# A hybrid decoder step on one core: the order of a tile's scores and transposes, of a few splits and of several loads is changed

## The chip, the core and the metric

The kernel runs on one core of a Trainium2 chip. The core has a matrix engine (TensorE, PE in the profile; its weight loads are PEld), three engines for element-wise work (VectorE, DVE; ScalarE, ACT; GpSimd, POOL), and SyncE (SP), which here only issues DMA transfers. Each engine works through its own queue in order, and semaphores hold an instruction until what it needs is there. The metric is the time of one execution on the device in microseconds; the lower, the better.

## The reference

One layer of a decoder, for a prompt of 2048 tokens and a sample batch of 8 x 8 tokens, d_model 1024, all in float32:

```python
h = rms_norm(x, g_mix_pre)
proj = einsum('btd,de->bte', h, w_in)            # q, k, v | gq, gk, gv, gr, low-rank gate
attn = swa_banded(rope(q), rope(k), v, sinks)    # window 128, 8 q heads, 2 kv heads, hd 64
log_a = log_sigmoid(glr @ w_gk2 + b_gk) / 16
o, s_new = gla_chunked(gq, gk, gv, log_a, s0)    # 4 heads, dk 64, dv 128
gla_out = rms_norm(o, g_gla) * silu(gr)
x = x + rms_norm(concat(attn, gla_out) @ w_out, g_mix_post)
h = rms_norm(x, g_ffn_pre)
f = relu(h @ w_up) ** 2 @ w_down                 # d_ff 4096
x = x + rms_norm(f, g_ffn_post)
```

The key and value windows and the recurrent states are returned too.

## The kernel before

**Precision.** TensorE multiplies in a rounded float32 format (float32r). So every operand is split in two: a high part (ScalarE copies with rounding) and a low part (VectorE subtracts the high part from the source). A product is three matmuls: high x high, high x low, low x high. Most lines of the profile that read `hi` and `lo`, `o0` and `o1`, `wh` and `wl`, `kh` and `kl`, `ph` and `pl` are such pairs.

**Order.** The program is fully unrolled. A scheduler places each engine's instructions, and takes from those that are ready the one that stands first in the text. Two things bind it. The wrappers `te`, `ac` and `dv` (class InOrder) keep every TensorE, ScalarE and VectorE instruction issued through them in the order of the text; plain `nc.scalar`, `nc.vector`, `nc.gpsimd` and `nc.sync` (DMA) calls may be placed earlier. And `tc.issue_after(ins)` puts what a block issues on the engine of `ins` behind `ins` in that engine's queue; it doesn't touch instructions of other engines. So a block of DMAs (SP) after a matmul (PE) is not bound by it, and one after a DMA is.

**Stages.** In order of time: sliding-window attention with its part of the input projection (to about 325 us of the span); gated linear attention with the rest of the projection; output projection, norms and residual; the up projection of the first half of the tokens (rows 0 to 1023 and the sample, `sb` = 0), the down projection of that half, and both again for the second half. Up and down are products of 2 x 2 blocks with seven instead of eight multiplications, so sums and differences of blocks are made on VectorE beside them.

**Attention.** The main loop runs over 16 tiles of 128 tokens (i), and in each over four units (u): a unit is two query heads of one key head. `unit` is a generator; each `next` issues one step:

1. the sink column (GpSimd); 2. scores `sc`, four matmuls; 3. mask and minimum (VectorE, `s<-sc,amask,sink`); 4. exponentials (ScalarE); 5. reciprocal (VectorE) and normalization, on VectorE, but in unit 3 on ScalarE (`s<-s,den`); 6. transposes `pT`; 7. `ph` (ScalarE); 8. `pl` (VectorE); 9. product with the values, `av`; 10. `rest` (ScalarE); 11. the addition `mo` (VectorE).

Tile 0 has one key block instead of two: step 10 then writes mo directly and there is no step 11. Three units are under way at a time: `behind` (steps 8 to 11), `now` (3 to 7), `ahead` (1 and 2). `fill` is the stream of projection matmuls that are put between them; A_FILL says how many where. The PSUM banks that matter: tag d (one buffer) holds the transposed queries pq of the next tile, and then the transposed inputs xT, which therefore wait for the last reader of pq, the `ql<-pq,ql` subtraction.

`heads_T` (L406) transposes the next tile's heads and returns pieces that A_PLAN places: `lo0` and `lo1` subtract the low parts of keys (`kl`, then GpSimd copies them to the other half) and queries (`qh`/`ql`) for each key head, `hi1` makes a high part. `rest` and `vl` in the plan are take_rest (L345) and its subtractions: `qk`, `glr`, `vv` on ScalarE, then `vv`, `glr` on VectorE. `split_some` splits weights of the next stage, of which a GpSimd product, a ScalarE copy and a GpSimd subtraction are made for each; A_SPLIT says how many in which unit. After tile 15 come four sample units (L531).

**Gated attention.** `decays` (L945) makes the log decays (Abs, Exp, Ln on ScalarE), `level_sums` sums them in seven levels, `gate` (L961) makes the output gate with four ScalarE activations. `gla` yields numbers: so many matmuls of `fill` (the remaining projection) are issued there.

**Output projection.** L1527 goes through the tiles in B_ORDER. `load_mix` loads a tile's mixed inputs `mt` into one of two buffers and splits them.

**Up projection.** `up` (L1612) takes 16 chunks of w_up. For the first one `opening` (L1731) lays the splits and sums by hand between the products; `last_rows` is the residual of the last tile. `sum_down` (L1600) makes differences of w_down blocks in two halves a chunk, placed by DOWN_SUMS and `downs`. `sample_features` at the end of a chunk reads the bank `sam` into `samq`.

**Down projection.** `down` (L1945) goes through 7 x 16 units: each loads two raw operands (`down_raw`: `rs` from s_d, `rt` from t_d or w_down, three buffers each), splits them (`o0`, `o1`) and does 12 matmuls `dn`. `fetch_h` and `load_h` bring the joint inputs H of the second half in meanwhile, `finish` and `prepare_last` end the rows.

Of the kernel before, what the change touches and what calls it, by code (L numbers as in the profile page):

```python
# [21 lines left out]
P = 128  # L22
# [29 lines left out]
DOWN_SUMS = (4, 6, 8, 10)  # L52
# [5 lines left out]
A_LEAD, A_SPLIT, A_PL_FIRST = 14, (2, 1, 0, 0), ()  # L58
A_PLAN = [(name, (int(at[0]), at[1])) for name, at in dict(
    first="1B", hi1="3B", x1="1B", lo1="0A", x0="0C", rest="3A", lo0="3A", junk="2A", turn="1A", rstd="1A", vl="3B"  # L60
# [80 lines left out]
def hybrid_step_kernel(ctx: ExitStack, tc: tile.TileContext, I, O):  # L141
# [264 lines left out]
    def heads_T(i):  # L406
# [36 lines left out]
        def lo(r):  # L443
            dv.tensor_tensor(kl[half_of[r], r, 1, :], pk[half_of[r]], f32(ks[half_of[r], r, 1, :]), op=ALU.subtract)
            nc.gpsimd.tensor_copy(kl[half_of[1 - r], r, 1, :], f32(kl[half_of[r], r, 1, :]))
            dv.scalar_tensor_tensor(
# [4 lines left out]
            "lo0": lambda: lo(0),  # L451
            "hi1": lambda: ac.activation(qs[1][half_of[1]], pq[half_of[1]], AF.Copy, scale=-0.125),
            "lo1": lambda: lo(1),
# [170 lines left out]
    def load_consts():  # L624
# [19 lines left out]
        def part(n, shape, dtype):  # L644
# [3 lines left out]
            nc.vector.tensor_copy(t.rearrange("p a b -> p (a b)") if len(shape) > 1 else t, src)  # L648
# [136 lines left out]
    for i in range(NB):  # L785
# [34 lines left out]
        for u in range(4):  # L820
            for unit_ in (behind, now) if u in A_PL_FIRST else (now, behind):
                next(unit_, None)
            next(now)
            do(u, "A")
            later = next(queue)
# [3 lines left out]
            next(behind, None)  # L829
# [9 lines left out]
            if u == 3:  # L839
                next(now)  # L840
                next(behind, None)
                next(ahead)
            else:
                next(behind, None)
                next(ahead)
                next(now)
            do(u, "B")
            split_some(A_SPLIT[u] if i < NB - 1 else 1)
# [96 lines left out]
    def decays(i, n, before, kind="d"):  # L945
# [12 lines left out]
        nc.scalar.activation(t, t, AF.Ln, bias=1.0)  # L958
# [122 lines left out]
    def gla(i, gp, og=iter(())):  # L1081
# [9 lines left out]
        yield G_FILL[0] if i else 24, True  # L1091
# [18 lines left out]
        sg = gate(i, gp, P)  # L1110
# [248 lines left out]
    wo, pre, ogs_of, mixes, late_mix, put = {}, {}, {}, {}, [], []  # L1359
# [5 lines left out]
    for i in range(NB):  # L1365
        parts = [gla(i, gps[i], ogs_of.pop(i - 1, iter(())))]
        if i == 0:
            parts = [(n or (12, True) for n in decayed(i)), *parts]
# [158 lines left out]
    for n, i in enumerate(B_ORDER[2:]):  # L1527
        early.append((i, []))
        mixing = out_projecting(nc.tensor, i, early[-1][1])
        run(mixing, 24 if i == B_ORDER[-1] else 48)  # L1530
        if n == 0:
# [80 lines left out]
    def up(sb, fc, before, steps=iter(())):  # L1612
# [62 lines left out]
        def downs(p):  # L1675

            if sb == 0 and fc > 1 and p in ((1, 2, 4) if fc in DOWN_SUMS else (1, 2)):
                sum_down(*next(down_halves))
# [52 lines left out]
    def opening(p, taken, ahead):  # L1731
# [5 lines left out]
        elif p == 2:  # L1737
            taken(p)
            next(last_rows)
            run(load_h(0, 6, ac, dv))  # L1740
            U.pop("tmp").release()
        elif p == 8:
            taken(p)
            sums_24(0, 0, dv)
            split_sums(0, 0, 24, ac, dv)
# [49 lines left out]
    def down_raw(sb, p, fc, which):  # L1795
# [10 lines left out]
        nc.sync.dma_start(raw, src)  # L1806
# [138 lines left out]
    def down(sb):  # L1945
# [28 lines left out]
        for n, (p, fc) in enumerate(units):  # L1974
# [3 lines left out]
            if sb == 0 and (p, fc) in fetched:  # L1978
                fetch_h(1, fetched[p, fc])
# [141 lines left out]
```

## Time and profile before

| | us |
|---|---|
| median of 3 runs | 2227.38 (2225.35 to 2230.99) |
| profiled execution | 2234.79 |
| its span, first to last instruction | 2233.0 |
| mean granted TensorE clock | 0.993 |
| ScalarE, VectorE and GpSimd busy | 1219.5, 1521.8, 261.0 |
| DMA | 419.92 MB, 188 GB/s over the span |

A row of the timeline reads: start, duration, engine, line, operation, out<-in by the program's names, shapes, count, and in brackets the idle time of the engine just before and what ended it. Most operations run through a helper, and so carry line L130; they are told apart by their tiles. A row of the list of waits reads: who waited for whom, the sum in us, how often, the longest. Matmuls are pipelined: successive starts tell how long one occupies the array, durations overlap.

### The profile page before, as it was taken

The page shows a single profiled execution, that of the slowest core. Times are in us where ns is not written, and L with a number is a line of the kernel's source. Part 1 is how long each engine was busy: PE and PEld are TensorE (multiplying, and loading weights), DVE is VectorE, ACT ScalarE, POOL GpSimd, SP SyncE. Part 2 cuts the span into 40 slices and gives each one's busy share as a digit, 9 for nine tenths or more (in the row PEclk, how much of TensorE's full clock was granted, in tenths as well). Part 3 has the DMA queues.
Part 4 walks back from the last instruction along what each step waited for, and adds up shares of the span by engine and source line. Part 5 has one row for each costly group of instructions (what it writes and reads, how often), then busy time and mean ns, then how long its engine had stood idle before and what let it go on. Part 6 is the DMA issues. An engine that isn't in the chain of part 4 may idle for free.

```text
span 2233.0 us, 34187 instructions
## 1 busy us (share of the span) xinstructions
PE 2174.4 (97%) x11784; PEld 1868.1 (84%) x11784; DVE 1521.8 (68%) x3101; ACT 1219.5 (55%) x2626; POOL 261.0 (12%) x417
## 2 busy tenths in 40 slices
PE   8999999999999999999999999999999999999998
PEld 7888888999998887788888778888888888888886
DVE  5778866777876565788888755447776666555566
ACT  5788866556665444455555554335454444454444
POOL 3566422111121110000000000000000000000000
PEclk9999999999999999999999999999999999999999
DMA  7334332124346559967786887557644444766674
GB/s 234 120 125 138 103 103 69 50 85 140 112 149 211 192 177 314 311 225 253 263 271 235 279 272 233 184 182 240 206 168 155 156 156 146 266 200 194 197 255 151
DMA packets 242313, 419.92 MB, mean 188 GB/s; under 512 B 26132, under 2 KB 142332, under 8 KB 238028
## 3 DMA queue, kind: packets, MB, share of 16 engines
q1 hardware_dynamic: 242140, 417.74, 56.0%
q8 instruction: 93, 1.52, 0.3%
q14 instruction: 80, 0.66, 0.1%
HBM read 270.53 MB, written 148.18 MB: 188 GB/s over the span
## 4 chain that ended last, share of the span: by engine, by line
PE 77%; ACT 7%; DVE 7%; DMA 5%; issue 2%; POOL 0%; SPq 0%; DVEq 0%; ACTq 0%; POOLq 0%
PE dn L130 24%; PE gproj L130 9%; PE uc L130 7%; PE ua L130 7%; PE out L1269 6%; PE ub L130 4%; PE ud L130 4%; PE ue L130 4%; PE proj L130 2%; ACT s L130 2%; PE sam L130 1%; PE dsam L130 1%; PE o L130 1%; DMA rt<-t_d 1%; DVE s L130 1%
## 5 line engine op out<-in xcount | busy, mean ns | idle before, releaser
L130 PE MATMUL dn<-o0t,o0s 128*128 128x512 f32 x896 | 350.1, 391 | 2.5 <-DVE samq L130 1.9
L130 PE MATMUL dn<-o1t,o0s 128*128 128x512 f32 x896 | 350.7, 391 | 1.6 <-DVE o1t L219 1.6
L130 PE MATMUL dn<-o0t,o1s 128*128 128x512 f32 x896 | 349.8, 390 | 0.0
L219 DVE TENSOR_TENSOR o1s<-rs,o0s 128x512 fp32r<-128x512 f32 x224 | 154.7, 691 | 234.9 <-ACT o0s L218 230.9
L218 ACT ACTIVATE o0s<-rs 128x512 fp32r<-128x512 f32 x224 | 141.1, 631 | 300.7 <-PE dn L130 278.1
L130 PE MATMUL gproj<-wg,gx 128*128 128x384 f32 x1408 | 265.7, 342 | 2.7 <-ACT dec L1025 1.8
L130 PEld LDWEIGHTS gproj<-wg,gx 128*128 128x128 f32 x1408 | 241.8, 189 | 7.8 <-issue 4.2
L130 ACT ACTIVATE st<-st 128x512 f32<-128x512 f32 x224 | 141.2, 630 | 138.0 <-DVE st L130 134.0
L130 PEld LDWEIGHTS dn<-o0t,o0s 128*128 128x128 f32 x896 | 168.5, 188 | 40.6 <-issue 2.3
L130 PEld LDWEIGHTS dn<-o1t,o0s 128*128 128x128 f32 x896 | 168.6, 188 | 39.8 <-DVE o1t L219 4.0
L130 PEld LDWEIGHTS dn<-o0t,o1s 128*128 128x128 f32 x896 | 168.6, 188 | 35.1
L130 PE MATMUL uc<-H,s 128*128 128x512 f32 x768 | 186.6, 391 | 0.0
L130 PE MATMUL ua<-H,w 128*128 128x512 f32 x744 | 179.2, 390 | 0.0
L130 PEld LDWEIGHTS uc<-H,s 128*128 128x128 f32 x768 | 143.4, 188 | 30.5
L130 PEld LDWEIGHTS ua<-H,w 128*128 128x128 f32 x744 | 139.6, 188 | 29.5
L1269 PE MATMUL out<-wo,mt 128*128 128x512 f32 x680 | 158.9, 392 | 1.6 <-ACT mt L218 1.5
L219 DVE TENSOR_TENSOR o1t<-rt,o0t 128x512 fp32r<-128x512 f32 x224 | 153.5, 685 | 9.4 <-ACT o0t L218 9.3
L208 POOL TENSOR_TENSOR frs<-rs_v,half 128x1 f32<-128x1 f32 (+1 forms) x13 | 10.0, 779 | 1213.8 <-DMA rt<-t_d 604.4
L1269 PEld LDWEIGHTS out<-wo,mt 128*128 128x128 f32 x680 | 126.5, 188 | 28.2 <-ACT mt L218 1.7
L218 ACT ACTIVATE o0t<-rt 128x512 fp32r<-128x512 f32 x224 | 138.5, 618 | 16.3 <-DMA rt<-t_d 15.4
L130 DVE TENSOR_TENSOR st<-st 128x512 f32<-128x512 f32 x160 | 110.6, 691 | 26.9 <-ACT st L130 22.7
L130 ACT ACTIVATE s<-t 128x1024 fp32r<-128x1024 f32 x62 | 65.8, 1061 | 97.6 <-PE ud L130 28.5
(393 smaller groups left out, 4232.9 us busy)
## 6 DMA issues: line engine op xcount, KB each, us to landing
s_d<-st SPq DMA_DIRECT2D x32, 1792.0 KB, 8.7
rs<-s_d SPq DMA_DIRECT2D x224, 256.0 KB, 3.2
raw<-in_w_up SPq DMA_DIRECT2D x64, 512.0 KB, 4.6
rt<-t_d SPq DMA_DIRECT2D x128, 256.0 KB, 3.4
rt<-in_w_down SPq DMA_DIRECT2D x96, 256.0 KB, 2.9
t<-in_w_down SPq DMA_DIRECT2D x64, 256.0 KB, 3.9
t_d<-t SPq DMA_DIRECT2D x32, 512.0 KB, 3.3
gx<-xt_d SPq DMA_DIRECT2D x28, 512.0 KB, 5.6
```

The lines of the kernel that those rows point to most:

```text
L130: ins = call(*a, **k)
L208: nc.gpsimd.tensor_tensor(out, v[:n], e, op=ALU.pow)
L218: nc.scalar.activation(hi, src, AF.Copy)
L219: vector.tensor_tensor(lo, src, f32(hi), op=ALU.subtract)
L1269: te.matmul(banks[c], x, w[:, c * 512 : (c + 1) * 512], start=k + u == 0, stop=k == KT - 1 and u == len(products) - 1,)
```

## The change

- DOWN_SUMS takes six chunks instead of four; `downs` makes no differences in the last chunk.
- The low part of key head 0 is a step of its own, `klo0`, placed in phase T of unit 3, a new phase between the mask step and `behind`'s pl. The query part stays in phase A.
- The main loop always takes `now` ahead of `behind` (as it did). In unit 0 the weight splits stand behind phase A instead of phase B. In unit 3 `behind`'s step 10 stands behind `now`'s normalization instead of ahead of the second fill, and the scores of `ahead` come ahead of `now`'s transposes.
- Three constant copies go from VectorE to GpSimd.
- `decays` keeps its last activation in `logs`; the gate of prompt tiles is issued behind it. At the start of gated attention the fills 12 and 24 become 4 and 32.
- In the output projection the next tile's `load_mix` stands behind the present tile's products, ahead of the residual that runs beside them; before, it stood at the start of the next tile's products, behind that residual.
- In `opening`, the sums and splits `24` stand at product 2 and the load of H part 6 at part 8, the other way round than before.
- In `down`, `latest` is the last raw load instead of the last matmul; the fetch of H, and the gains' load, are put behind it, as are the `x1` loads that named `latest` already.

```diff
-DOWN_SUMS = (4, 6, 8, 10)
+DOWN_SUMS = (3, 5, 7, 9, 11, 13)
...
-A_LEAD, A_SPLIT, A_PL_FIRST = 14, (2, 1, 0, 0), ()
+A_LEAD, A_SPLIT = 14, (2, 1, 0, 0)
...
-    first="1B", hi1="3B", x1="1B", lo1="0A", x0="0C", rest="3A", lo0="3A", junk="2A", turn="1A", rstd="1A", vl="3B"
+    klo0="3T", first="1B", hi1="3B", x1="1B", lo1="0A", x0="0C", rest="3A", lo0="3A", junk="2A", turn="1A", rstd="1A", vl="3B"
...
-        def lo(r):
+        def k_lo(r):
             dv.tensor_tensor(kl[half_of[r], r, 1, :], pk[half_of[r]], f32(ks[half_of[r], r, 1, :]), op=ALU.subtract)
             nc.gpsimd.tensor_copy(kl[half_of[1 - r], r, 1, :], f32(kl[half_of[r], r, 1, :]))
+
+        def q_lo(r):
             dv.scalar_tensor_tensor(
                 qs[r][half_of[1 - r]], pq[half_of[r]], -0.125, f32(qs[r][half_of[r]]), op0=ALU.mult, op1=ALU.subtract
             )
...
-            "lo0": lambda: lo(0),
+            "klo0": lambda: k_lo(0),
+            "lo0": lambda: q_lo(0),
...
-            "lo1": lambda: lo(1),
+            "lo1": lambda: (k_lo(1), q_lo(1)),
...
-            nc.vector.tensor_copy(t.rearrange("p a b -> p (a b)") if len(shape) > 1 else t, src)
+            nc.gpsimd.tensor_copy(t.rearrange("p a b -> p (a b)") if len(shape) > 1 else t, src)
...
         for u in range(4):
-            for unit_ in (behind, now) if u in A_PL_FIRST else (now, behind):
-                next(unit_, None)
+            next(now)
+            do(u, "T")
+            next(behind, None)
             next(now)
             do(u, "A")
+            if u == 0 and i < NB - 1:
+                split_some(A_SPLIT[u])
             later = next(queue)
             next(later)
             run(fill, A_FILL[u][0])
             next(behind, None)
-            next(behind, None)
+            if u != 3:
+                next(behind, None)
             run(fill, A_FILL[u][1])
...
             next(now)
             if u == 3:
-                next(now)
                 next(behind, None)
-                next(ahead)
-            else:
-                next(behind, None)
-                next(ahead)
-                next(now)
+            next(behind, None)
+            next(ahead)
+            next(now)
             do(u, "B")
-            split_some(A_SPLIT[u] if i < NB - 1 else 1)
+            if u or i == NB - 1:
+                split_some(A_SPLIT[u] if i < NB - 1 else 1)
...
-        nc.scalar.activation(t, t, AF.Ln, bias=1.0)
+        logs[:] = [nc.scalar.activation(t, t, AF.Ln, bias=1.0)]
...
-        yield G_FILL[0] if i else 24, True
+        yield G_FILL[0] if i else 32, True
...
-        sg = gate(i, gp, P)
+        with tc.issue_after(logs[0].ins):
+            sg = gate(i, gp, P)
...
-            parts = [(n or (12, True) for n in decayed(i)), *parts]
+            parts = [(n or (4, True) for n in decayed(i)), *parts]
...
         run(mixing, 24 if i == B_ORDER[-1] else 48)
+        if n + 3 < len(B_ORDER) and B_ORDER[n + 3] not in mixes:
+            mixes[B_ORDER[n + 3]] = load_mix(B_ORDER[n + 3])
...
-            if sb == 0 and fc > 1 and p in ((1, 2, 4) if fc in DOWN_SUMS else (1, 2)):
+            if sb == 0 and 1 < fc < NFC - 1 and p in ((1, 2, 4) if fc in DOWN_SUMS else (1, 2)):
...
         elif p == 2:
             taken(p)
             next(last_rows)
+            sums_24(0, 0, dv)
+            split_sums(0, 0, 24, ac, dv)
+        elif p == 8:
+            taken(p)
             run(load_h(0, 6, ac, dv))
             U.pop("tmp").release()
-        elif p == 8:
-            taken(p)
-            sums_24(0, 0, dv)
-            split_sums(0, 0, 24, ac, dv)
...
-        nc.sync.dma_start(raw, src)
+        latest[:] = [nc.sync.dma_start(raw, src)]
...
             if sb == 0 and (p, fc) in fetched:
-                fetch_h(1, fetched[p, fc])
+                with tc.issue_after(latest[0].ins):
+                    fetch_h(1, fetched[p, fc])
...
-                done = products(n, j)
-            latest[:] = [done]
+                products(n, j)
...
             if n == 26:
-                with tc.issue_after(done.ins):
+                with tc.issue_after(latest[0].ins):
                     gains_post(sb)
```

More of the change, by code (lines that the diff above doesn't have):

```diff
@@ L1357, in mixed @@
         nc.sync.dma_start(x1_d[i], x[:n])
[L1359 removed]
+    wo, pre, ogs_of, mixes, late_mix, put, logs = {}, {}, {}, {}, [], [], []
     wo_parts = iter(())
```

## The prediction

> **What bounds the kernel now.** I read the page's busy shares first, then the list of who waited for whom on TensorE, then sums by stage, then the timeline around each long wait.
>
> ```profile
> PE 2174.4 (97%) x11784; PEld 1868.1 (84%) x11784; DVE 1521.8 (68%) x3101; ACT 1219.5 (55%) x2626; POOL 261.0 (12%) x417
> rs<-s_d SPq DMA_DIRECT2D x224, 256.0 KB, 3.2
> ...
> PE pT L130 <- ACT s L130: 15.4, 16, 1.4
> PE ua L130 <- ACT s L130: 3.0, 1, 3.0
> PE dn L130 <- DVE samq L130: 1.9, 1, 1.9
> PE gproj L130 <- ACT dec L1025: 1.8, 1, 1.8
> ...
> PE out L1269 <- ACT mt L218: 1.5, 1, 1.5
> ...
> PE ssc L130 <- ACT kc L130: 1.2, 2, 0.7
> ...
> 54.86:58.28 3.42, 3.42 (x14) 3.42 (x13) 2.63 (x9) 1.63 (x6) 3.28 (x5) 0.50 0.08 27
> 317.69:321.10 3.41, 3.41 (x22) 3.24 (x15) 2.35 (x8) 1.33 (x5) 0.00 (x0) 0.50 0.47 135
> ...
> 420.09:423.50 3.41, 3.41 (x53) 2.97 (x54) 1.78 (x4) 0.58 (x1) 0.00 (x0) 0.50 0.65 187
> ...
> 932.09:938.91 6.82, 6.18 (x14) 4.40 (x15) 3.34 (x4) 2.95 (x5) 0.00 (x0) 0.50 1.02 406
> ...
> 1270.01:1273.42 3.41, 3.41 (x9) 2.64 (x8) 2.18 (x4) 2.40 (x5) 0.00 (x0) 0.50 0.85 302
> ...
> 975.00:1250.00 275.00, 275.00 (x1320) 230.56 (x1319) 227.37 (x366) 149.14 (x247) 0.00 (x0) 1.00 0.74 254
> ```
>
> TensorE is the bound, so only its waits can be won. The largest group is one wait in each of the 16 attention tiles (15.4 us). In the window rows the columns are length, then busy time of PE, PEld, DVE, ACT and POOL, then the granted clock, DMA share and GB/s. Five stretches shown run at a granted clock of 0.50, four of them behind waits of the list (tile 0's, the last tile's, ua's and dn's); such a stretch of 3.41 us does half its work and so costs up to 3.41 / 2 = 1.7 us on top of the wait. The last row has TensorE busy for all of its 275 us: in the up projection nothing is to be won.
>
> **Scores ahead of the transposes (tiles 1 to 14).** One boundary between two tiles, as the timeline has it:
>
> ```profile
> 104.66 0.69 DVE L130 TENSOR_TENSOR pl<-pT,ph 128x512 fp32r<-128x512 f32 x1 [0.47 <-ACT ph L130]
> ...
> 105.27 0.27 DVE L130 TENSOR_TENSOR kl<-pk,kh 64x128 fp32r<-64x128 f32 x1
> ...
> 105.98 0.35 PE L130 MATMUL proj<-wa_lo,xh 128*128 128x392 f32 x1
> 106.03 0.37 ACT L130 ACTIVATE vv<-proj,rstd_all 128x128 fp32r<-128x128 f32 x1
> ...
> 106.29 0.17 DVE L130 RECIPROCAL den<-den 128x2 f32<-128x2 f32 x1
> 106.42 0.38 ACT L130 ACTIVATE rest<-av 64x256 f32<-64x256 f32 x1
> 106.71 0.90 ACT L130 ACTIVATE s<-s,den 128x256 f32<-128x256 f32 x2
> 106.83 0.42 DVE L130 TENSOR_TENSOR mo<-av,rest 64x256 f32<-64x256 f32 x1 [0.38 <-ACT rest L130]
> ...
> 107.26 0.84 PE L130 MATMUL pT<-ident,s 128*128 128x128 f32 x4 [0.93 <-ACT s L130]
> 107.27 0.35 DVE L130 SCALAR_TENSOR_TENSOR vv<-proj,rstd_all,vv 128x128 fp32r<-128x128 f32 x1
> 107.53 0.22 DVE L130 SCALAR_TENSOR_TENSOR glr<-proj,rstd_all,glr 128x16 fp32r<-128x16 f32 x1
> ...
> 107.85 0.36 PE L130 MATMUL sc<-kh,qh 128*128 128x256 f32 x1
> ...
> 108.41 0.34 PE L130 MATMUL proj<-wa_hi,xl 128*128 128x392 f32 x1
> ...
> 108.61 0.48 DVE L130 CUSTOM_DVE_ANT_0 s<-sc,amask,sink 128x256 f32<-128x256 f32 x1 [0.85 <-PE sc L130]
> ...
> 109.42 0.69 DVE L130 TENSOR_TENSOR pl<-pT,ph 128x512 fp32r<-128x512 f32 x1
> ...
> 110.46 0.69 DVE L130 SCALAR_TENSOR_TENSOR ql<-pq,ql 64x512 fp32r<-64x512 f32 x1
> ...
> 111.21 0.42 PEld L130 LDWEIGHTS xT<-ident,x 128*128 128x128 f32 x4 [0.19 <-DVE ql L130]
> ```
>
> Replayed in the new order: the key subtraction (0.27) moves into the 0.47 us in which VectorE waits ahead of pl, so the reciprocal is ready 0.3 sooner. ScalarE's two normalizations no longer stand behind rest: they start when vv ends, 106.03 + 0.37 = 106.40 instead of 106.71. The transposes, 0.55 behind them as now (107.26 - 106.71), start at 106.95. The four scores, which take 108.41 - 107.85 = 0.56, fit in from about 106.16 on (one matmul behind 105.98). The transposes issue in 107.85 - 107.26 = 0.59, so the next projection starts at 107.54, **0.87 sooner** than 108.41.
>
> Where the stall goes: rest now stands behind the normalizations on ScalarE, and mo, vv, glr and the next tile's first mask step stand behind rest on VectorE. rest ends at 106.40 + 0.90 + 0.38 = 107.68 at most, mo starts 0.03 later as now (106.83 against 106.42 + 0.38), vv 0.44 behind mo, glr 0.26 behind vv, and the mask step 0.22 behind glr: 108.63, against 108.61 now. If rest overlaps its predecessor by 0.1, it is 108.53. From there VectorE runs without a gap through pl to the ql subtraction that ends at 111.15, and the input transposes wait for that one (the last row: 111.21, released by ql). TensorE comes sooner and waits there, and at the matmuls on pl just ahead. So 0.87 is won and lost again: I take **0 for these 14 tiles**, with 0.1 per tile to either side, -1.4 to +1.4.
>
> **First and last tile.** Tile 0 has one key block and so no rest and no mo addition: nothing is moved behind the normalization that VectorE needs. Its wait is the longest (1.4), and the half-clock stretch at 54.86 follows it. Bounds: 0.87 as above, and 1.4 + 1.7 = 3.1; with the transposes held by the normalization still, I take -1.8. At the last tile the unit ahead is a sample unit, whose four cache-key transposes take the scores' place; its later wait for kc (0.7) goes with them, and 317.69 is at half clock too. Bounds 0.5 (four transposes at 0.59 / 4, with an overlap lost) and 0.7 + 1.7 = 2.4: -1.5. No trace shows whether the clock then stays up; hence values nearer the middle.
>
> **Weight splits moved ahead in unit 0.** In tiles 4 to 10 they fill ScalarE's gaps. In tile 3 the multiplication by GpSimd that they need may be late, and rest and the input copy then queue behind it. Both ways a wait of one pair of activations and its product is at stake; from the largest wait of TensorE for an activation queued behind others (1.8, gproj's) I bound it at -2 to +2 and take 0. The three constant copies that go to GpSimd (12% busy) are hidden behind its idle time: 0, and a fraction of a microsecond if not.
>
> **Gated attention's start.** Fills 12/24 become 4/32, and the gate's activations go behind the next decay's logarithm. The same count of matmuls, the first decays about 8 fills sooner; the gate's four activations land in a busier ScalarE stretch, where the gp evictions queue behind them and TensorE behind those. At stake is gproj's wait for dec, 1.8. The other way, the gate's four activations of 128x512 become a new wait: each takes at least one 128x256 normalization (0.90 / 2 = 0.45) and at most two (0.90), +1.8 to +3.6. I take -1.2, and -1.8 and +2.4 as ends, since much of ScalarE's queue there can be passed.
>
> **Mixed inputs a tile ahead.** The 1.5 us wait goes, or stays where another load stands ahead in SP's queue: -1.5 to +1.5, taken -1.2 since the wait is met from its own side. In the text the load passes one residual, and so on SP that residual's input load and its stores; they are covered by being needed a tile later, and without that cover a wait like this one, +1.5, moves to the residual.
>
> **Opening of the up projection.**
>
> ```profile
> 924.78 1.28 DVE L130 SCALAR_TENSOR_TENSOR x<-bx,bssq,gpre 128x1024 f32<-128x1024 f32 x1 [0.66 <-POOL bssq L208]
> ...
> 927.90 1.06 ACT L130 ACTIVATE H<-hraw 128x1024 fp32r<-128x1024 f32 x1 [0.62 <-DMA hraw<-h_d]
> ...
> 928.99 1.23 DVE L130 TENSOR_TENSOR H<-hraw,H 128x1024 fp32r<-128x1024 f32 x1 [0.45 <-ACT H L130]
> 929.28 0.44 PE L130 MATMUL sam<-ident,both 128*128 128x128 f32 x2 [0.51 <-ACT both L130]
> ...
> 930.85 0.69 DVE L130 TENSOR_TENSOR t<-raw,t 128x512 f32<-128x512 f32 x1
> 931.58 1.06 ACT L130 ACTIVATE s<-t 128x1024 fp32r<-128x1024 f32 x1 [2.35 <-DVE t L130]
> ```
>
> Product 6 needs s (now from 932.64) and H of part 6. New order on VectorE from 926.06: two sums (1.4) to 927.5, s high on ScalarE to 928.5, s low to 929.75, then H low behind it, one 1.23 after the other: the first half at about 931.0. So H takes the place of s, and the product starts at 931.0, 1.7 sooner. The half clock (6.82 us, up to 3.4) may go with it or not. Bounds 0 and 1.7 + 3.4 = 5.1; I take -2.5.
>
> **From up to down, first half.** The change leaves no differences of w_down for the last chunk, and queues the joint inputs' fetches behind a down load.
>
> ```profile
> 1248.62 1.91 SPq L1481 DMA_DIRECT2D hraw<-h_d  x2
> ...
> 1256.55 0.32 SPq L1806 DMA_DIRECT2D rs<-s_d  x1
> ...
> 1262.49 0.63 ACT L218 ACTIVATE o0s<-rs 128x512 fp32r<-128x512 f32 x1 [0.53 <-DMA rs<-s_d]
> ```
>
> Now two fetches for the second half stand in the queue ahead of the first down operand, which lands 5.9 us after its issue (1262.49 - 1256.55) where the page has 3.2. Behind it come the splits, the three sums and samq, for which TensorE waits 1.9. With the fetches ordered behind, it may land up to 2.7 sooner; the wait and its half-clock stretch go: 1.9 + 1.7 = 3.6 at best, 0 at worst. I take -2.8. The differences, dealt to six chunks instead of four, lie beside a TensorE that is never idle (the 275 us row): 0. In the down stage itself the order edges cost or save single waits below 1 us: -1 to +2, taken 0.
>
> **Sum.** -1.8 - 1.5 - 1.2 - 1.2 - 2.5 - 2.8 = -11.0. The profiled execution took 2234.79 us (span 2233.0), so 2223.8 on its scale. The median of the runs, 2227.38, is 7.4 lower; taken off that, **2216 us**, -0.5%. All best ends together (-1.4 - 3.1 - 2.4 - 2 - 1.8 - 1.5 - 5.1 - 3.6 - 1 = -21.9) give 2205.5, all worst (+1.4 - 0.9 - 0.5 + 2 + 2.4 + 1.5 + 0 + 0 + 2 = +7.9) give 2235.3.
>
> **Rivals.**
> 1. The tiles' gain is kept. If rest ends early enough that VectorE's chain moves with the scores, 14 x 0.87 = 12.2 more: 2204. For it: the mask step now waits 0.85 for the scores. Against: the replay puts rest in that gap.
> 2. The waits change places: H, the gp eviction and the first down operand stay as late, and only the two end tiles and the mixed inputs gain, -4.5: 2223. For it: product 6 has a second operand in line; against: 1.7 us by rows.
> 3. The half clock doesn't come from the waits and stays. Of the sum, about 0.9 at tile 0, 0.7 at the last tile, 0.8 at the opening and 1.4 at the change to down rest on it, 3.8: 2220. For it: the stretch at 420.09 has no wait of the list ahead of it. Against it: the four others have. The Trainium skill ("TensorE: Matmul & The Clock Gate", "Why this matters for your kernels") asks for no idle gap over about 3 us; by that rule the 1.4 and 1.9 us waits would not halve the clock, and the sum would be this rival's. The rows disagree: 0.50 follows both.
> 4. Slower. The seven joint fetches are now held until the down stage, between raws that TensorE needs soon. If each delays the raws behind it by the 2.7 us above beyond their cover, and costs 1.7 of half clock with it, that is 7 x 2.7 = 19 to 7 x 4.4 = 31: 2235 to 2247, 2238 as its value. It decides where a raw comes later than the two units of loads ahead of TensorE, 2 x 12 matmuls, cover. Against it: the raws land in 3.2 us at the median.
>
> **How the numbers follow.** Forecast 0.45, rival 1 0.13, rival 2 0.18, rival 3 0.11, rival 4 0.13. The forecast's own range is 2208 to 2222. The whole range must reach rivals 1 and 2 and stop short of 4: 2203 to 2232. 0.3% of 2227.4, about what this measurement can tell from no change, is 6.7 us: under 2220.7 is faster, over 2234.1 slower. Faster: nearly all of the forecast (0.42), rival 1 (0.13) and over half of 3 (0.07): 0.62. Slower: rival 4 and 0.01 of the rest: 0.14. Between: rival 2 and what is left, 0.24.
>
> **What would show it.** In the new profile the transposes' wait at ScalarE's s should fall from 15.4 to under 5 us; in its place waits of av for pl and of xT for ql should come, some 0.8 us a tile, and a tile should still take about as long. Product 6 should wait for H low. samq's wait should be gone and 1270 at full clock. I am wrong in the main step if the tiles get 0.5 us shorter or more, and wrong in sign if dn matmuls wait for down operands.

## The result, and the profile after

The changed kernel takes 2249.56 us (median of 4 runs, 2249.43 to 2255.1), the kernel before 2229.18 in the same comparison: a ratio of 1.0096, 95% interval 1.0069 to 1.0123. It is **slower by about 1%**; the forecast was 2216. The profiled execution spans 2247.6 us against 2233.0, and the mean granted clock is the same (0.994 and 0.993), so the time did not go to the clock.

Busy times after, and then who waited for whom on TensorE (engine, line, released by; sum in us, times, longest):

```profile
PE 2182.1 (97%) x11784; PEld 1866.9 (83%) x11784; DVE 1533.1 (68%) x3098; ACT 1213.3 (54%) x2626; POOL 261.6 (12%) x420
```

```profile
PE o L130 <- DVE S L1152: 6.6, 8, 1.3
...
PE av L130 <- DVE pl L130: 5.2, 19, 0.3
PE o L130 <- ACT AT L1148: 4.4, 3, 1.9
PE uc L130 <- DMA H<-hp_d: 4.1, 2, 3.4
PE xnT L1461 <- DVE x L1451: 3.8, 2, 2.8
PE proj L130 <- ACT qk L130: 2.7, 5, 0.7
...
PE dsam L130 <- DVE fs L1831: 2.4, 1, 2.4
PE av L130 <- ACT ph L130: 2.2, 1, 2.2
...
PE ssc L130 <- ACT kc L130: 1.1, 2, 0.6
...
PE dn L130 <- DVE samq L130: 0.2, 1, 0.2
PE pT L130 <- ACT s L130: 0.2, 1, 0.2
```

Read against the list of before: the waits that the change aimed at are gone. The transposes' wait for the normalized scores fell from 15.4 to 0.2, samq from 1.9 to 0.2, and ua's wait for s isn't in the list any more. One that the forecast also counted on is still there: the sample units' wait for kc (1.2 before, 1.1 now). Most of the lines above these are new or have grown (before, o waited 2.2 for S and 1.3 for AT, xnT 1.2 for x, av 1.2 for ph); the experiments tie them to different parts of the change.

To see where the time went, one takes rows that mark a stage and compares their first and last start. These are four rows of the view by tile, before and then after: the attention transposes pT, the first products of gated attention gl, the residual's transposes xnT in the output projection, and the down products dn (first and last start follow the three durations).

```profile
L130 PE MATMUL pT<-ident,s x248: 270/273/332, 42.5 to 315.9; 128*128 128x128 f32 x124
...
L130 PE MATMUL gl<-XQ,kt x128: 222/222/369, 371.5 to 721.3; 128*64 128x64 f32 x128
...
L1455 PE MATMUL xnT<-ident,x x128: 222/272/299, 750.2 to 914.7; 128*128 128x128 f32 x120, 64*128 64x64 f32 x8
...
L130 PE MATMUL dn<-o0t,o0s x896: 387/389/628, 1265.8 to 2223.3; 128*128 128x512 f32 x180
```

```profile
L130 PE MATMUL pT<-ident,s x248: 270/273/421, 42.6 to 321.4; 128*128 128x128 f32 x124
...
L130 PE MATMUL gl<-XQ,kt x128: 222/222/369, 371.8 to 733.4; 128*64 128x64 f32 x128
...
L1461 PE MATMUL xnT<-ident,x x128: 222/272/447, 762.1 to 931.1; 128*128 128x128 f32 x120, 64*128 64x64 f32 x8
...
L130 PE MATMUL dn<-o0t,o0s x896: 387/389/503, 1281.7 to 2237.9; 128*128 128x512 f32 x180
```

The attention tiles lose 5.5 (321.4 - 315.9). The stretch from there to the first gl wins that back: gl starts only 0.3 later. **Gated attention loses 12** (361.6 from first to last gl against 349.8). The output projection loses another 4.4 (169.0 against 164.5). From there on the delta stays near 15.

Inside the attention the loss is not even. The timeline gives the length of a tile, counted here and below from the transposes of its unit 3 to those of the next tile:

| tile | before | after |
|---|---|---|
| 1, 2 | 17.39, 17.40 | 17.04, 17.03 |
| 3 | 19.02 | 22.07 |
| 4 to 8 | 17.39 to 17.41, two 17.16 | 18.78 to 18.98 |
| 9 to 11 | 17.40 to 17.44 | 17.02 to 17.05 |

Tiles in which no weights are split got **0.36 us shorter**; those with splits 1.5 us longer, and the first of them 3. Of these 3 us, some 1.7 belong to a stretch of 3.41 us at half clock that follows the wait there (from 116.40 on; before has none in this tile).

### The profile page after: what moved, and what is told of

It is laid out like the page before. It is cut to its first block, busy times and chain, and to the rows that moved or that the text cites. A ratio compares the mean times of both kernels' runs of the same rounds, so it can differ in the third digit from the quotient of the medians.

```text
span 2247.6 us, 34125 instructions
## 1 busy us (share of the span) xinstructions
PE 2182.1 (97%) x11784; PEld 1866.9 (83%) x11784; DVE 1533.1 (68%) x3098; ACT 1213.3 (54%) x2626; POOL 261.6 (12%) x420
## 5 line engine op out<-in xcount | busy, mean ns | idle before, releaser
L130 PE MATMUL dn<-o1t,o0s 128*128 128x512 f32 x896 | 349.8, 390 | 1.4 <-DVE o1t L219 1.4
```

Source lines behind the costliest of these rows:

```text
L130: ins = call(*a, **k)
```

## The experiments

### The new order of unit 3 by itself

The kernel before with the main loop's new order and klo0, all else as before:

```diff
-            for unit_ in (behind, now) if u in A_PL_FIRST else (now, behind):
-                next(unit_, None)
+            next(now)
+            do(u, "T")
+            next(behind, None)
...
-            next(behind, None)
+            if u != 3:
+                next(behind, None)
...
             if u == 3:
-                next(now)
                 next(behind, None)
-                next(ahead)
-            else:
-                next(behind, None)
-                next(ahead)
-                next(now)
+            next(behind, None)
+            next(ahead)
+            next(now)
```

> The kernel before with the new order of unit 3 alone (scores of the unit ahead before the transposes, rest behind the normalization, the key subtraction of head 0 in phase T); splits, loads, edges and fills as before. Before: 2229.2. Theory: tile 0 gains about 2 us, tiles 1 to 14 0.37 each, the last tile and the sample units some 3 to 5 more: 2217 to 2223, with the transposes' wait for the normalized scores nearly gone. The prediction's own steps: 0 for tiles 1 to 14, so -3.3: 2226. Rival: the new order costs the tiles with weight splits, which stand in GpSimd's and ScalarE's queues in tiles 3 to 10, as much as it wins: 2229 to 2233.

Measured: 2222.74 against 2229.03, ratio 0.9971 (0.9960 to 0.9982). A tile takes 17.03 to 17.04, also with splits (tile 7: 17.29; tile 3: 18.83, before 19.02). So this part wins 6.3 us, and the rival falls. One boundary of this kernel in the timeline:

```profile
138.90 0.37 ACT L130 ACTIVATE vv<-proj,rstd_all 128x128 fp32r<-128x128 f32 x1
...
139.16 0.91 ACT L130 ACTIVATE s<-s,den 128x256 f32<-128x256 f32 x2
...
139.73 0.84 PE L130 MATMUL pT<-ident,s 128*128 128x128 f32 x4
...
140.10 0.38 ACT L130 ACTIVATE rest<-av 64x256 f32<-64x256 f32 x1
...
140.51 0.42 DVE L130 TENSOR_TENSOR mo<-av,rest 64x256 f32<-64x256 f32 x1 [1.38 <-ACT rest L130]
...
141.35 0.48 DVE L130 CUSTOM_DVE_ANT_0 s<-sc,amask,sink 128x256 f32<-128x256 f32 x1
...
142.90 0.45 PE L130 MATMUL av<-pl,vv 128*64 128x256 f32 x2 [0.26 <-DVE pl L130]
```

The mechanism is the one that was replayed: rest behind the normalization, mo 0.03 behind rest, a new wait for pl (0.26). But VectorE's chain ends a little sooner, not at the same time: from the end of ScalarE's vv copy (138.90 + 0.37 = 139.27) the mask step starts 2.08 later, where the replay had 2.23 and before had 2.21.

### The weight splits in unit 0

The changed kernel with the splits behind phase B again:

```diff
-            if u == 0 and i < NB - 1:
-                split_some(A_SPLIT[u])
...
-            if u or i == NB - 1:
-                split_some(A_SPLIT[u] if i < NB - 1 else 1)
+            split_some(A_SPLIT[u] if i < NB - 1 else 1)
```

> The changed kernel with the weight splits of unit 0 behind phase B again. Theory: the splits in front of the input copy and rest on ScalarE cost the attention tiles 3 to 8, about 2.4 + 5 x 1.7 = 11 us; without them tiles 3 to 8 keep the 0.4 us a tile that tiles 1 to 2 gain, so 2249.6 - 11 - 2 = 2236 to 2240. Rival: the tiles with splits lose because the new order of unit 3 leaves VectorE and ScalarE no slack beside any split, wherever it stands; then 2247 to 2251 and the projection matmuls still wait for qk there.

Measured: 2238.03, ratio 1.0039 (1.0024 to 1.0054), 11.5 us less than the changed kernel; tiles with splits take 17.04 again. So the place of the splits costs 11.5 us. Why, the changed kernel's timeline tells (GpSimd, ScalarE and TensorE rows of one tile):

```profile
135.03 0.83 POOL L261 TENSOR_TENSOR wg_raw<-wg_raw,gcol 128x384 f32<-128x384 f32 x1 [1.61 <-DMA wg_raw<-in_w_in]
...
136.31 0.83 POOL L261 TENSOR_TENSOR wg_raw<-wg_raw,gcol 128x384 f32<-128x384 f32 x1 [0.46 <-DMA wg_raw<-in_w_in]
...
137.10 0.55 POOL L208 TENSOR_TENSOR rstd_all<-rs_v,half 128x1 f32<-128x1 f32 x1
...
137.68 0.59 ACT L130 ACTIVATE qk<-proj,rstd_all 128x392 f32<-128x392 f32 x1 [2.32 <-POOL rstd_all L208]
...
138.32 0.44 PE L130 MATMUL proj<-wa_hi,xh 128*128 128x392 f32 x1 [0.74 <-ACT qk L130]
```

Read it from below: TensorE waits for the eviction qk, ScalarE for the row scale rstd_all, and this power of 128 x 1 stands on GpSimd behind two products for the *next* tile's splits, which wait there for their raw weights. The same two kinds of row in the run with the new order alone stand the other way round, with the power first:

```profile
130.69 0.56 POOL L208 TENSOR_TENSOR rstd_all<-rs_v,half 128x1 f32<-128x1 f32 x1
132.42 0.83 POOL L261 TENSOR_TENSOR wg_raw<-wg_raw,gcol 128x384 f32<-128x384 f32 x1 [1.18 <-DMA wg_raw<-in_w_in]
```

An earlier split frees its raw buffer earlier, so the next load goes out earlier (in these two tiles 5.9 us behind the transposes of unit 3 instead of 7.1), and the product that needs it moves up on GpSimd, past the power. To test that, the changed kernel with the early splits kept, and only the product issued behind the power (`roots` collects the powers of the tiles' normalizations):

```diff
-        nc.gpsimd.tensor_tensor(raw, raw, gcol[:, k : k + 1].to_broadcast([P, G_N]), op=ALU.mult)
+        with tc.issue_after(roots[-1].ins):
+            nc.gpsimd.tensor_tensor(raw, raw, gcol[:, k : k + 1].to_broadcast([P, G_N]), op=ALU.mult)
```

> The changed kernel, its weight splits still ahead in unit 0, but the GpSimd product that each split begins with is issued behind the last GpSimd power of the tiles' normalization (rstd). Theory: the splits cost 11.5 us not on ScalarE but on GpSimd: products that wait for their raw weights (1.6 + 0.5 in a tile) stand ahead of the 128x1 power, the projection's eviction on ScalarE waits 2.3 for that, and TensorE for the eviction; with the power first a tile takes 17.0 to 17.1 again and the time is 2237 to 2240. Rival: the splits' copies ahead of rest and the input copy on ScalarE are what costs; then a tile with splits still takes 18.8 to 19.0 and the time stays at 2247 to 2252.

Measured: 2241.4, ratio 1.0053 (1.0040 to 1.0065). Tiles 4 to 8 take 16.9 to 17.3, and TensorE's waits for qk between 120 and 235 us are gone. ScalarE's waits in that stretch, first in the changed kernel and then here:

```profile
ACT qk L130 <- POOL rstd_all L208: 10.3, 5, 2.3
```

```profile
ACT ph L130 <- PE pT L130: 4.7, 13, 1.3
```

So 8.2 of the 11.5 us hang on the order of two instructions on GpSimd. The rest is tile 3, which still takes 22.80: there, in the changed kernel, the split's copy on ScalarE waits 3.61 us for a product that GpSimd reaches only after the rotation, and rest and the input copy stand behind that copy:

```profile
110.97 0.53 ACT L130 ACTIVATE wg<-wg_raw 128x384 fp32r<-128x384 f32 x1 [3.61 <-POOL wg_raw L261]
```

With the power first, 6.83 us at half clock follow this wait, so that some 3.4 of the 4.0 us between 22.80 and 18.83 are the clock's in that execution.

### The gate behind the logarithm

The edge taken out of the changed kernel, and put alone into the kernel before:

```diff
-        with tc.issue_after(logs[0].ins):
-            sg = gate(i, gp, P)
+        sg = gate(i, gp, P)
```

> The changed kernel without the edge that puts the gate's activations behind the next decay's logarithm; the fills 4 and 32 stay. Changed kernel: 2249.6 us, before: 2229.2. Theory: the edge costs the steady tiles of gated attention, where the delta to before grows by 12.4 us (from +0.2 to +12.6), since the gate's activations and its GpSimd products now run among the level sums and make the attention matrix late; without it 10 to 13 us go, so 2237 to 2240, and the waits of o for AT in the tiles from the fifth on fall back to those of before. Rival: the fills 4/32 shift all of the stage; then it stays at 2247 to 2251.

> The kernel before with the gate's edge alone (its activations behind the next decay's logarithm), fills 12 and 24 as before. Theory: the edge by itself costs the steady tiles of gated attention 10 to 13 us: 2239 to 2242, and o waits for AT or S in most tiles from the fifth on. Rival: it costs only with the fills 4 and 32: 2228 to 2231. The prediction: -1.8 to +2.4 around 2229.

Measured: 2244.19 without it (ratio 1.0067, 1.0053 to 1.0081), so 5.4 less than the changed kernel; 2236.91 with it alone (1.0036, 1.0022 to 1.0050), so 8.2 more than before. The stage shows both, first without the edge and then with it alone: 349.6 and 360.4 us from first to last gl, where before has 349.8 and the changed kernel 361.6.

```profile
L130 PE MATMUL gl<-XQ,kt x128: 222/222/369, 377.0 to 726.6; 128*64 128x64 f32 x128
```

```profile
L130 PE MATMUL gl<-XQ,kt x128: 222/222/271, 366.2 to 726.6; 128*64 128x64 f32 x128
```

The edge costs some 11 us in this stage; that its own removal wins only 5.4 has to do with the start: without it gl comes 5.2 later (1.9 of that from the attention before), and TensorE waits 2.7 us there for gp_s. All sixteen profiles agree on this: from the last pT to the first gl it is 50.2 to 50.9 us in the eight with the edge, without half clock, and 52.4 to 55.6 in the eight without it (1.4 to 6.1 us at half clock in six of them), whatever the order of unit 3. So, with the products on GpSimd, the edge wins 2 to 5 us ahead of the first gl and loses 10 to 12 behind it. Beside a tile's level sums the changed kernel's timeline shows (VectorE and GpSimd):

```profile
565.95 0.29 DVE L1034 TENSOR_TENSOR before<-before 128x128 f32<-128x128 f32 x1
566.52 1.30 POOL L975 TENSOR_TENSOR sg<-sg,gp 128x512 f32<-128x512 f32 x1 [9.56 <-ACT sg L974]
566.83 1.14 DVE L1033 TENSOR_TENSOR after<-after,before 128x128 f32<-128x128 f32 x1 [0.58 <-ACT dec L1032]
567.90 1.27 POOL L977 TENSOR_TENSOR sg<-sg,ggla 128x512 f32<-128x512 f32 x1
568.00 1.31 DVE L1034 TENSOR_TENSOR before<-before 128x128 f32<-128x128 f32 x1
569.42 0.29 DVE L1033 TENSOR_TENSOR after<-after,before 128x128 f32<-128x128 f32 x1
```

A sum of 0.29 us takes 1.14 and 1.31 while GpSimd runs the gate's two products: each ends some 0.15 behind the product beside it (566.52 + 1.30 = 567.82 against 567.97; 567.90 + 1.27 = 569.17 against 569.31). In the kernel before, the first of these products ran in a gap of 1.76 us in which VectorE waited for zt, and only one sum was stretched, to 0.81:

```profile
556.34 1.30 POOL L970 TENSOR_TENSOR sg<-sg,gp 128x512 f32<-128x512 f32 x1 [5.21 <-ACT sg L969]
557.71 1.29 POOL L972 TENSOR_TENSOR sg<-sg,ggla 128x512 f32<-128x512 f32 x1
...
557.88 0.42 DVE L959 SCALAR_TENSOR_TENSOR before<-z,zt 128x256 f32<-128x256 f32 x1 [1.76 <-ACT zt L958]
558.34 0.81 DVE L1028 TENSOR_TENSOR after<-after,before 128x128 f32<-128x128 f32 x1
```

The Trainium skill ("SBUF — State Buffer", "SBUF: two separate sides") says that a VectorE instruction with two inputs from SBUF and a GpSimd instruction that reads SBUF exclude each other for a whole instruction, the one that starts later being held until the other ends; the rows agree. As the test, the kernel before with the edge, and the two products on VectorE:

```diff
-        nc.gpsimd.tensor_tensor(t[:n], t[:n], gr, op=ALU.mult)
+        nc.vector.tensor_tensor(t[:n], t[:n], gr, op=ALU.mult)
...
-        nc.gpsimd.tensor_tensor(t4, t4, ggla[:n].unsqueeze(1).to_broadcast([n, 4, P]), op=ALU.mult)
+        nc.vector.tensor_tensor(t4, t4, ggla[:n].unsqueeze(1).to_broadcast([n, 4, P]), op=ALU.mult)
```

> The kernel before with the gate's edge (2236.9 us), and the gate's two products of 128x512 on VectorE instead of GpSimd. Theory: with the edge these two products, 1.3 us each on GpSimd, run beside the level sums, and VectorE's additions of two operands from SBUF are held up by them (mean 0.32 us before, 0.41 with the edge); off GpSimd the mean is 0.32 to 0.33 again, and though VectorE gets two operations of about 0.7 us per tile more, the time comes down to 2229 to 2234. Rival: the edge costs through ScalarE's order (the exponentials of the level sums come behind the gate's four activations); then the time stays at 2236 or more, VectorE's two operations coming on top.

Measured: **2219.8**, ratio 0.9960 (0.9946 to 0.9974): 17.1 us less than with the products on GpSimd, and 9 to 10 less than before. One of the two sums between 400 and 700 us (busy, mean ns), before, in the changed kernel and in this run:

```profile
L1028 DVE TENSOR_TENSOR after<-after,before 128x128 f32<-128x128 f32 x92 | 29.8, 324 | 8.3 <-ACT dec L1027 2.3
```

```profile
L1033 DVE TENSOR_TENSOR after<-after,before 128x128 f32<-128x128 f32 x89 | 36.0, 405 | 7.8 <-ACT dec L1032 3.9
```

```profile
L1028 DVE TENSOR_TENSOR after<-after,before 128x128 f32<-128x128 f32 x91 | 26.4, 290 | 3.9 <-ACT dec L1027 0.8
```

The mean is 324 before, 405 changed, 290 here (417 with the edge and the products on GpSimd), and the stage takes 343.1 us (gl from 367.4 to 710.5). That the time falls below the expected 2229 to 2234 fits this: the sums are shorter than before, too. TensorE's waits for S and AT between 385 and 705 us, 9.3 in the changed kernel and 3.5 before, come down to 0.2. The rival, ScalarE's order, falls.

Three more runs follow. The first is the version that the runs so far point to, with the new order of unit 3 as well; the second asks whether the edge still matters then, and the third how far this carries over to the changed kernel:

> The kernel before with the new order of unit 3 (alone 2222.7 us), the gate's edge, and the gate's two products on VectorE (these two together 2219.8). Theory: the two gains lie in different stages and add up, 6.3 to 6.5 and 9.2 to 10.4: 2212 to 2215. Rival: the runs with both parts gain the start of gated attention twice (its half-clock stretches went in either), so some 4 us less: 2216 to 2219.

> As the run with both, without the gate's edge. Theory: the products on GpSimd cost by running beside VectorE's sums, wherever the scheduler puts them; off GpSimd the edge is worth little: within 3 us of the run with both. Rival: without the edge the gate's activations and the two products stand early on ScalarE and VectorE, ahead of the decays and the sums, so it is 4 to 10 us slower than the run with both.

> The changed kernel with the gate's two products on VectorE instead of GpSimd, all else as changed. Theory: what the edge lost in the steady tiles was GpSimd beside the level sums, so the delta of gated attention (from +0.2 to +12.6) turns to -4 to -6 as in the kernel before: 2249.6 - 17 = 2231 to 2234. Rival: with the fills 4/32 and the other handover the waits for AT stay: 2240 or more.

| | median us | ratio to before (95%) | first to last gl |
|---|---|---|---|
| order, edge, products on VectorE | **2216.95** | 0.9939 (0.9926 to 0.9951) | 344.5 |
| the same without the edge | 2219.57 | 0.9952 (0.9938 to 0.9966) | 345.3 |
| changed, products on VectorE | 2234.46 | 1.0022 (1.0012 to 1.0031) | 345.0 |

The best version is 12.9 us faster than before; the sum of the two gains would have been 2212 to 2215, so some 3 us were counted twice, as the rival had it. The edge is then worth 2.6 by the medians, with intervals that overlap; it no longer costs. So the cost was the products' place beside the sums, not the gate's place in ScalarE's queue. In the changed kernel the two lines win back 15.1.

### The mixed inputs a tile ahead

The early load taken out; then, in the kernel without the edge and the moved splits, the residual's input issued ahead of it:

```diff
-        if n + 3 < len(B_ORDER) and B_ORDER[n + 3] not in mixes:
-            mixes[B_ORDER[n + 3]] = load_mix(B_ORDER[n + 3])
```

```diff
+        if n > 1 and early[0][0] not in res_x:
+            res_x[early[0][0]] = load_x(early[0][0])[0]
         if n + 3 < len(B_ORDER) and B_ORDER[n + 3] not in mixes:
```

> The changed kernel without the load of the mixed inputs a tile ahead in the output projection (it stands at the start of the tile's own products again). Theory: the load, passed over a residual, delays that residual's own input and shifts the last residuals, whose transposes then wait 2.8 us with a half-clock stretch behind; the stage lost 3.8 us (delta +12.6 to +16.4); without it 2245 to 2247 and a wait of the products for mt of about 1.5 comes back. Rival: the stage's loss comes from what lies before it (the timing with which gated attention hands over); then 2249 to 2251.

> The changed kernel without the gate's edge and the moved splits, with the mixed inputs still loaded a tile ahead, but the residual's own input issued ahead of that load. Theory: what the early load costs is the residual's input, which stands behind it in SP's queue while it waits for its buffer (5 us later than before); with the input ahead of it the 2.8 us wait of the residual's transposes goes, and so does the wait for mt (1.5 with half clock behind): 1 to 4 us below the kernel with the three undone, 2217 to 2221. Rival: the early split of the mixed inputs itself, which stands ahead of the residual on ScalarE and VectorE, makes the residual late: then about 4 us above it, 2224 to 2227.

Measured: 2245.88 without it (1.0076, 1.0061 to 1.0091), 3.7 us less than changed, and the mt wait of 1.3 is back. SP's queue in the changed kernel shows the cause:

```profile
883.30 0.59 SPq L1475 DMA_DIRECT2D h_d<-ht  x1
887.59 0.92 SPq L1249 DMA_DIRECT2D mt<-mix_d  x1
888.55 1.50 SPq L1428 DMA_DIRECT2D bx<-in_x_prompt  x1
```

SP stands for 3.7 us (883.89 to 887.59) in front of the mt load, until TensorE is through with the products that read its buffer (xnT follows them at 887.40), and the residual's bx stands behind it. Without the early load bx goes out at 883.10, in a run whose stage begins within 0.4 us of this one. The residual's transposes then wait 2.8 and bring half-clock windows. With bx first the time is 2224.42, the same as the 2224.48 of the kernel without any early load (below). So the 3.7 us seem to go with the order on SP (the early load without bx ahead of it was not run in this kernel), but nothing is won, against the expectation of 2217 to 2221: a wait of products for the residual's x (2.0) takes the place of the one for mt (1.6). It is not settled which of the early split's two instructions is in the way there.

### What is left: fills, opening, fetches

The changed kernel with gate edge, splits and mixed inputs undone; then with the opening undone too; then, instead, with the order of the fetches undone:

> The changed kernel without the gate's edge, without the splits moved and without the load of the mixed inputs a tile ahead; the new order of unit 3, the fills, the opening, the differences and the order of the joint fetches stay. Theory: the three cost about 5 + 11 + 4 = 20 us of the changed kernel's 2249.6; what is left is the new order of unit 3 (2222.7 alone against 2229.0 before), with at most 2 from the change to the down projection: 2220 to 2224. The prediction's own sizes for what is left (opening 2.5, change to down 2.8): 2217 to 2218. Rival: the three overlap (the gate's edge also shortens the start of gated attention), so undoing all of them gives less than the sum: 2225 to 2230.

> The kernel with the three undone, and in the opening of the up projection the sums and the load of H of part 6 back in their old places. Theory: the swap is worth nothing: the wait for s (2.96) goes and a wait for H from hp_d (3.4 + 0.7) comes in its place, since these loads start 3 us later; so within 2 us of the kernel with the three undone, with the s wait of 2 to 3 back and the hp_d wait below 2. The prediction's step: 2.5 us slower, up to 5.1.

> The kernel with the three undone (2224.5 us), and in the down projection the joint fetches, the gains and the x1 loads bound as before (to a matmul, so in effect free on SP's queue). Theory: the order of the fetches moves the samq wait (1.9) with what follows to a later wait of the sampled part for its own sums (2.4 at the last of the first half), so nothing is left: 2222 to 2227, with the samq wait of about 1.9 back. The prediction's step: 2.8 us slower, up to 3.6. The slower rival of the prediction (the bound fetches delay raw loads by 19 to 31 us): this kernel would be that much faster.

| | median us | ratio to before (95%) |
|---|---|---|
| three undone | 2224.48 | 0.9976 (0.9967 to 0.9985) |
| and the opening | 2224.33 | 0.9979 (0.9970 to 0.9988) |
| and the fetches instead | 2225.21 | 0.9981 (0.9972 to 0.9989) |

The three, and so all that is left beside the new order (2222.74), tell nothing apart. The differences of w_down and the constant copies were not taken out by themselves; whatever they do is within this. In the opening the stall changes its place: waits between 905 and 960 us with the swap (three undone) and without it:

```profile
PE uc L130 <- DMA H<-hp_d: 3.5, 2, 2.4
```

```profile
PE ua L130 <- ACT s L130: 3.0, 1, 3.0
```

TensorE starts product 6 sooner and meets H from hp_d, whose loads start later (946.33 in the changed kernel, 15.2 us behind the first up matmul; before 926.74, 12.0 behind). From up to down the samq wait is back with the fetches free (2.5), and nothing is lost by it: with the fetches bound, TensorE waits 3.1 for the sampled part's sums fs later on, which it doesn't with them free.

## Why the prediction was wrong

**Tiles 1 to 14** (0, with -1.4 to +1.4): the mechanism was right, the size not. The transposes' wait went and waits for pl (0.26) and ql (0.13) came, as replayed; but up to 0.36 a tile stays, so the term was -4 to -5 over the 14 tiles (242.9 us for them before, 238.8 with the new order alone). The replay took VectorE's chain to end where it ended before; its mask step comes 0.13 sooner (2.08 against 2.21 behind the vv copy), and it followed the tile no further than ql, behind which av's wait for rs_v (0.18 a tile before) is gone too. Rival 1 (all of 0.87 kept) is wrong too.

**First and last tile** (-1.8 and -1.5): right in size at tile 0, in part by luck; wrong at the last. Tile 0's wait of 1.4 went, and the changed kernel gains 2.0 there (16.27 against 18.31). But 1.5 of this is the half clock, which the old order has in two of its three profiles only: in the run with the edge alone tile 0 takes 16.78 at full clock, and the order then wins 0.5. At the last tile the step said that the wait for kc goes; it stayed (1.2 and 1.1), and the stretch that ends with this tile's last transposes gets 0.5 shorter (16.12 against 16.67). The 5.2 us between the last pT and the first gl (from +5.5 to +0.3) are the gate's edge and the half clock: with the new order alone that stretch takes 52.4 without any half clock, and before 55.6 with 6.06 us at half clock, 3.0 of which are lost, so 52.6 without.

**Weight splits moved** (0, with -2 to +2): this step failed, by 11.5 us. It named a late GpSimd product with rest and the input copy behind it, and that came (3 us, 1.7 of them the half clock), at the start of tile 4, which the table counts to tile 3. For the others it said that the splits fill ScalarE's gaps and looked at ScalarE alone. What was late next was on GpSimd, 12% busy: the split's first product moved up on GpSimd in front of the power that scales the rows. The step moved the copies and didn't follow that a split also frees a buffer, starts a load, and brings a product that waits for this load to the front of GpSimd's queue.

**Gated attention** (-1.2, with -1.8 to +2.4): the second failure, +5 to +8 us as measured. It priced the start alone, where the wait for dec (1.8) did go and 2 to 5 us were won, and not the tiles behind it, which each repeat the new order and lost 10 to 12. It saw a busier ScalarE; the cost was in the gate's two GpSimd products, which the list of parts did not contain at all. They came to lie beside VectorE's level sums.

**Mixed inputs** (-1.2, with -1.5 to +1.5): wrong in sign, +3.7. The step that it named as the danger, a wait that moves to the residual, is the one that happened; its price left out that SP stands still in front of a load whose buffer is not free.

**Opening** (-2.5): 0 measured (0.2 between two runs' medians). Here rival 2 was right: the waits change places. **Up to down** (-2.8): the samq wait did go (1.9 to 0.2), but a wait for fs came later on, and 0.7 is what the runs show of the gain, less than they can tell from none. **Rival 4**, the slower one, named the wrong place: no dn product waits long for an operand, and with the fetches free the time is the same.

**The half clock** (rival 3) is below. The sum of the parts as measured is, against 2229: order -6.3, opening, fetches and fills about +2 (or nothing), splits +11.5, gate +5.4, mixed inputs +3.7, that is 2245; the changed kernel's 2249.6 has some 4 us more, and the runs don't say between which of the parts these arise.

## What to carry to other kernels

GpSimd, at 12% busy, cost some 8 us through the order of two instructions and 17 us through two products that ran beside VectorE's sums: look at what stands behind an instruction on it that waits for a transfer, and what runs beside it. When an activation is moved, list the whole chain that moves with it, on every engine and in every repeated tile, not only at the first. And a load that waits for its buffer held up the loads behind it on SP's queue (3.7 us in the rows above), so the load that is needed first has to stand first.

## What the runs showed of the hardware

**VectorE and GpSimd.** A sum of 128 x 128 with both inputs in SBUF takes 0.29 us alone and up to 1.31 beside a GpSimd product (above). The same product of 128 x 512 took 1.30 us on GpSimd and 0.69 on VectorE.

**The half clock.** In each execution all stretches at 0.50 start on one grid of 3.413 us, whose position differs from run to run. Summed by windows of that grid, from the gaps between TensorE's records from 40 to 2200 us in all sixteen profiles, 42 of 43 full-clock windows with at least 1.9 us of idle time were followed by a window at 0.50; of 34 with 1.5 to 1.8 us it was 5, and of 83 with 0.9 to 1.2 none. So it is the idle time within one window that tells, and not the length of a wait: before, the samq wait of 1.94 lay in one window, and 0.50 followed; with the fetches free a longer one, 2.46, was cut by the grid into 1.77 and 0.69, and the clock stayed up (length, busy times, granted clock in the seventh place; the first row is the wait itself):

```profile
1257.01:1259.47 2.46, 0.00 (x1) 0.03 (x1) 2.28 (x5) 0.17 (x2) 0.00 (x0) 1.00 0.85 281
1259.47:1262.88 3.41, 3.41 (x15) 2.81 (x16) 2.18 (x4) 2.76 (x7) 0.00 (x0) 1.00 0.85 269
```

The forecast's 1.7 us behind waits of 1.4 come in some executions only and were thus too much, and the Trainium skill's 3 us ("TensorE: Matmul & The Clock Gate", "Why this matters for your kernels") is too long for these rows. The spread between executions goes with the clock: of 16 timed runs of the kernel before, those at a mean clock of 0.997 took 2223.2 to 2227.6 us, those at 0.993 and 0.994 2229.5 to 2232.9. The stretch at 420.09, and its like 47 to 52 us behind the first gl in ten of the sixteen profiles, have no idle TensorE in the records ahead of them. There the sample part's sixteen matmuls with only 16 columns, and eight of 64 x 64, stand close together: in these ten, one window holds at least 14 of the sixteen and two of the eight, and 0.50 follows it; in the other six the grid parts the two groups or the sixteen, and no half clock follows. So they seem to count as idle; no run changed them to test it.
